# Input projection of a diffusion block: the order of weight loads, of the modulation's dot products and of the first tile

## The chip, the cores and the metric

The kernel runs on one core of a Trainium2 chip. Its time is the device time of one execution in microseconds (us); smaller is better. Runs of the kernel before are summed up by their median. The engines are named as the profile names them: PE multiplies matrices (PEld is its weight load), DVE and ACT work elementwise, POOL is the fourth compute engine, and SP issues transfers, which 16 DMA engines carry out. On-chip memory is SBUF (data) and PSUM (matmul results).

## The reference

One block of a diffusion transformer on 512 latent tokens and 256 context tokens, width 2048, all in float32. Cut to what the change touches:

```python
mod_l = silu(c) @ w_ada + b_ada            # 6 x 2048 values
mod_c = silu(c_ctx) @ w_ada + b_ada        # the same for the context
sh_a, sc_a, gt_a, sh_f, sc_f, gt_f = split(mod_l, 6)
h_l = rms_norm(x, g_mix) * (1 + sc_a) + sh_a       # 512 x 2048
h_c = rms_norm(ctx, g_mix) * (1 + csc_a) + csh_a   # 256 x 2048
p_l = h_l @ w_in                           # 2048 x 3904: query, key/value, rotary key, conv
p_c = h_c @ w_in                           # only its key/value columns are read later
# attention of latent tokens over latent and context keys; gated convolution of width 3
x = x + gt_a * (merge(att, conv) @ w_out)  # the output projection
x = x + gt_f * conv_ffn(modulate(rms_norm(x)), w_up, w_down)
out = rms_norm(x, g_final)
```

## The kernel before

Activations lie transposed: a tile holds 128 of the 2048 features (k = 0 to 15) by 512 tokens. Every product is made of three matmuls, high x high, high x low and low x high (`mm3`, L180), since each operand is split into a rounded high part (a cast on ACT) and the rest (a subtraction on DVE). For weights that is `split` (L156), with its cast at L164 and its low part at L165; for activations it is `hilo` (L312), at L315 and L316.

The input projection has 31 column tiles of 128 and goes through k in three chunks of 2, 4 and 10 tiles (`KCH`, index `ci`). Within a chunk, the first six column tiles (`G`) are worked row by row into six PSUM halves (`pf`), so that they can begin as soon as one k tile exists; the remaining 25 follow one by one (`pp`), and each is added to its sum `acc` by `evac` (ACT copies in the first chunk, L517; DVE adds later, L519). PSUM gives these tiles four single banks and two double ones in turn (`bank`). Weights arrive as `rf` (768 KB, for the six first tiles and two k) and `rw` (up to 1024 KB); both use the `raw` tag with two buffers, and their split parts `wh` and `wl` have four buffers and a spare for every fifth.

A tile of h (`prep`, L406) needs two values per feature out of w_ada: `mods` (L402) loads two tiles of w_ada for the scale (t = 16 + j) and for the shift (t = j), each as two halves 128x1024 (`ada`, 512 KB each, four buffers), and DVE multiplies each half by the vector `sv` (silu(c), on all 128 partitions) and sums it in one instruction (`dot_v`, L227). `modulate` (L410) then multiplies x by the norm's reciprocal root `rl`, and applies scale and shift on ACT (L416). Tiles 0 and 1 are made ahead of their matmuls in the first chunk, the others between column tiles by the table `todo`.

The norm's sum of squares is one chain of 16 additions on DVE (`add_squares`, L333). PE sums it over partitions (`rs`, L298), ACT takes the root (L275), DVE the reciprocal (L277), PE spreads it (L282), and ACT copies it to `rl` (L305). The vectors silu(c) and silu(c_ctx) come through `silu_rows` (L383): an 8 KB row is loaded, four matmuls against ones spread it over the partitions, and four Silu activations write `sv` or `svc`. ACT loads another function table (ACT_TABLE_LOAD) when it goes from Silu to the square root.

The context's scales and shifts are the same dots with `svc` (`ctx_mods`, L498, dots at L508): 32 steps of two dots, taken by `next(cm)`: one at each of the ten k rows of the third chunk's first tiles, then one at each following column tile and two at every fourth. `ctx_prep` (L483) makes two context tiles each from the results; `ctx_tile` (L659) multiplies them by w_in's key/value columns after the latent tokens are done (weights `wc`, PSUM `pc`).

A scheduler orders each engine's instructions with a timeline of its own; `keep` fixes some in program order. `fetch_to` (L141) keeps all loads on SP's queue in program order until the second chunk's first tiles are done (`ordered[0] = False`). SP issues one transfer after the other, and a load waits at the queue's head until its buffer is free. A weight load of `load` (L147) is written where its tile is wanted. `sv` is also stored to DRAM (`sv_d`, 1 MB), to be read back in the last part of the kernel. The output projection (around 640 to 700 us) also has a first part worked row by row with weights `ofr` (768 KB, split parts `ofw`), while `x` tiles are loaded again by `x_tile` (L947).

## Time and profile before

| | |
|---|---|
| time, median of 3 runs | 2158.85 us (2157.04 to 2159.15) |
| profiled execution's own time | 2154.39 us |
| its span in the trace | 2152.4 us |
| granted clock, mean | 0.995 |
| PE busy | 2092.9 us, 97% |
| DVE busy | 1770.2 us, 82% |
| ACT busy | 1047.3 us, 49% |
| first matmul of the projection | 30.12 us |
| first matmul of the second chunk | 85.19 us |
| first matmul of the third chunk | 170.24 us |

A row of a timeline reads: start, duration, engine, line, operation, result<-operands, and in brackets the idle time before it with what ended it. A row of waits reads: who waited, <-, for whom, then us in total, times, longest. SPq is SP's queue of issues. The profiled execution is one run; its time lies 4.5 us under the median.

### The profile page before, as it was taken

To read this page: it belongs to the slowest core of one execution; us is meant where nothing else is said; L and a number is where in the kernel's file an instruction comes from. 1 tells how busy PE (TensorE), PEld (TensorE's weight loads), DVE (VectorE), ACT (ScalarE), POOL (GpSimd) and SP (SyncE) were. 2 spreads that over 40 slices of the span, in tenths; PEclk is the share of its full clock that TensorE was granted. 3 is DMA by queue.
4 is the path that set the end of the run, shared out by engine and by line. 5 is a ranking of instruction groups with operands and counts; after the bars stand their busy time and mean duration, and the time that the engine had idled before them with its cause. 6 is when DMAs were issued, how large, how long until landed. Compare 5 with 4: busy or idle time off the path is not lost.

```text
span 2152.4 us, 37747 instructions
## 1 busy us (share of the span) xinstructions
PE 2092.9 (97%) x14458; PEld 1936.3 (90%) x14458; DVE 1770.2 (82%) x2859; ACT 1047.3 (49%) x1709; POOL 188.6 (9%) x270
## 2 busy tenths in 40 slices
PE   7899999999999999999999999999999989999997
PEld 4688788888888888999999999999999869999997
DVE  7998987778886989788888878888888658888886
ACT  5533333555552337555555555555555424333445
POOL 0000000000000000111211211211111000000000
PEclk9999999999999999999999999999999999999998
DMA  9989785334559976677877877887887998888782
GB/s 332 346 276 333 272 281 177 130 124 166 167 197 350 373 272 192 159 215 202 242 224 222 241 221 226 241 238 216 245 233 222 350 329 246 272 222 241 207 253 96
DMA packets 162410, 513.89 MB, mean 239 GB/s; under 512 B 18995, under 2 KB 23347, under 8 KB 156595
## 3 DMA queue, kind: packets, MB, share of 16 engines
q1 hardware_dynamic: 132564, 417.10, 56.9%
q0 software_dynamic: 27488, 92.29, 18.3%
q8 instruction: 113, 1.85, 0.4%
q10 hardware_dynamic: 2176, 2.10, 0.3%
q14 instruction: 69, 0.56, 0.1%
HBM read 464.22 MB, written 46.14 MB: 237 GB/s over the span
## 4 chain that ended last, share of the span: by engine, by line
PE 88%; DMA 5%; DVE 4%; issue 1%; ACT 1%; SPq 0%; POOL 0%; DVEq 0%; ACTq 0%; POOLq 0%
PE pp L181 4%; PE pp L183 4%; PE pp L182 4%; PE o L181 1%; PE o L183 1%; PE o L182 1%; DMA ada<-in_w_ada 1%; PE uf L181 1%; PE uf L182 1%; PE uf L183 1%; PE of L181 1%; PE of L182 1%; PE of L183 1%; PE pf L182 1%; PE pf L183 1%
## 5 line engine op out<-in xcount | busy, mean ns | idle before, releaser
L1029 POOL DMA_DIRECT2D t_d<-tp x126 | 72.7, 580 | 461.6 <-DVE tp L1028 458.7
L249 DVE SCALAR_TENSOR_TENSOR ada<-ada,sv 128x1024 f32<-128x1024 f32 x68 | 82.0, 1218 | 13.1 <-DMA ada<-in_w_ada 13.1
L164 ACT CAST w_0h<-rw 128x512 fp32r<-128x512 f32 (+1 forms) x63 | 38.3, 618 | 108.0 <-PE pp L182 63.6
L1106 POOL DMA_DIRECT2D u_s<-in_w_up x80 | 70.3, 879 | 226.4 <-DMA u_s<-in_w_up 124.8
L227 DVE SCALAR_TENSOR_TENSOR ada<-ada,sv 128x1024 f32<-128x1024 f32 x64 | 77.4, 1217 | 3.8 <-DMA ada<-in_w_ada 3.6
L508 DVE SCALAR_TENSOR_TENSOR ada<-ada,svc 128x1024 f32<-128x1024 f32 x64 | 75.8, 1218 | 3.2 <-DMA ada<-in_w_ada 3.2
L1027 ACT CAST tp<-a 128x256 fp32r<-128x256 f32 x90 | 34.8, 406 | 66.5 <-DMA t_d<-tp 58.0
L771 POOL TENSOR_TENSOR gr<-gr,half 128x8 f32<-128x8 f32 x4 | 10.1, 2522 | 629.3 <-DVE gr L770 537.0
L165 DVE TENSOR_TENSOR w_0l<-rw,w_0h 128x512 fp32r<-128x512 f32 (+1 forms) x63 | 42.5, 680 | 21.8 <-ACT w_0h L164 21.6
L249 DVE SCALAR_TENSOR_TENSOR ra<-ra,sv 128x1024 f32<-128x1024 f32 x44 | 52.4, 1216 | 1.3 <-DMA ra<-in_w_ada 1.3
L1198 DVE TENSOR_TENSOR u<-u,u_s 128x1024 f32<-128x1024 f32 x40 | 48.8, 1219 | 1.2 <-DMA u_s<-in_w_up 1.2
L1199 DVE TENSOR_TENSOR u<-u,u 128x1024 f32<-128x1024 f32 x40 | 48.7, 1217 | 0.0
L1028 DVE TENSOR_TENSOR tp<-a,tp 128x256 fp32r<-128x256 f32 x90 | 36.1, 417 | 13.5 <-ACT tp L1027 13.3
L742 ACT CAST pth<-t 128x384 fp32r<-128x384 f32 x64 | 28.6, 485 | 26.3 <-PE t L739 26.3
L1027 ACT CAST tp<-ts 128x256 fp32r<-128x256 f32 x36 | 14.6, 407 | 44.0 <-DMA t_d<-tp 42.2
L1028 DVE TENSOR_TENSOR tp<-ts,tp 128x256 fp32r<-128x256 f32 x36 | 15.1, 421 | 25.2 <-ACT tp L1027 25.2
L519 DVE TENSOR_TENSOR acc<-acc,pp 128x512 f32<-128x512 f32 x50 | 34.0, 679 | 2.1 <-PE pp L183 2.1
L743 DVE TENSOR_TENSOR ptl<-t,pth 128x384 fp32r<-128x384 f32 x64 | 33.2, 548 | 2.7 <-ACT pth L742 2.7
L723 DVE TENSOR_REDUCE mn<-s 128x1 f32<-128x768 f32 x32 | 30.3, 951 | 4.8 <-PE s L712 4.6
L990 ACT ACTIVATE g<-cg,sm 128x512 f32<-128x512 f32 x40 | 32.5, 813 | 1.0 <-DVE cg L1167 0.9
L990 ACT ACTIVATE a<-ca,sm 128x512 f32<-128x512 f32 x40 | 32.1, 802 | 0.0
L1233 DVE SCALAR_TENSOR_TENSOR aq<-aq,svq 128x512 f32<-128x512 f32 x32 | 21.1, 688 | 12.6 <-DMA aq<-in_w_ada 11.2
(15965 smaller groups left out, 9380.6 us busy)
## 6 DMA issues: line engine op xcount, KB each, us to landing
ada<-in_w_ada SPq DMA_DIRECT2D x196, 512.0 KB, 5.8
u<-in_w_up SPq DMA_DIRECT2D x120, 512.0 KB, 8.2
w<-t_d SPq DMA_DIRECT2D x161, 256.0 KB, 4.3
u_s<-in_w_up SPq DMA_DIRECT2D x80, 512.0 KB, 4.2
u_s<-in_w_up POOLq DMA_DIRECT2D x80, 512.0 KB, 9.1
t_d<-tp POOLq DMA_DIRECT2D x126, 256.0 KB, 5.0
v<-in_w_dnw SPq DMA_DIRECT2D x72, 384.0 KB, 4.6
ra<-in_w_ada SPq DMA_DIRECT2D x22, 1024.0 KB, 4.9
```

The costliest lines, as they stand in the source:

```text
L181: PE.matmul(ps, w[0], x[0], start=first, stop=False, skip_group_check=on_top)
L182: PE.matmul(ps, w[0], x[1], start=False, stop=False, skip_group_check=on_top)
L183: PE.matmul(ps, w[1], x[0], start=False, stop=last, skip_group_check=on_top)
L227: V.scalar_tensor_tensor(out=r, in0=r, scalar=1.0, in1=vec[:, i * 1024:(i + 1) * 1024], op0=ALU.mult, op1=ALU.mult, accum_out=col[:, i:i + 1])
L249: keep(V.scalar_tensor_tensor(out=r, in0=r, scalar=1.0, in1=svs[i], op0=ALU.mult, op1=ALU.mult, accum_out=lc[:, t % 4:t % 4 + 1] if i else ...
L508: keep(V.scalar_tensor_tensor(out=raw[q], in0=raw[q], scalar=1.0, in1=svc[:, q * 1024:(q + 1) * 1024], op0=ALU.mult, op1=ALU.mult, accum_o ...
L990: A.activation(u, src, AF.Identity, bias=s("fb", m), scale=s("fw", 86 + m))
L1027: A.copy(out=z[:, :256], in_=src)
L1028: V.tensor_tensor(out=z[:, 256:], in0=src, in1=z[:, :256].bitcast(F32), op=ALU.subtract)
L1029: G_.dma_start(t_d[p, OPS.index(n)], z.bitcast(F32))
L1106: G_.dma_start(r[-1], src[more], accum_op=ALU.add)
L1198: V.tensor_tensor(out=a11, in0=a11, in1=s1, op=ALU.add)
```

## The change

Five things change.

1. The weight loads of the projection stand in a table, and `weights()` hands out the load that was issued one step earlier and issues the next. In the first chunk the next one is issued after the second tile's modulation loads.
2. The first tile has its own code. Its two pairs of w_ada tiles are loaded and the scale's dots (t = 16) come ahead of the reciprocal; the shift's dots (t = 0) are put around the multiplication by `rl`. The squares are summed in two chains of eight. Casts and low parts of the first weights are ordered after named instructions by `issue_after`, and the copy of `rl` comes ahead of the weights' casts.
3. The context's row is no longer loaded at the beginning and spread by matmuls. In the second chunk, after the first tiles, c_ctx is loaded to all 128 partitions (1 MB) and one Silu of 128x2048 makes `svc`.
4. The context's dots: one step at the first eight rows of the third chunk's first tiles, then one at each column tile. `ctx_prep` begins two tiles later.
5. The store of `sv` goes from the beginning to the output projection, behind the seventh x tile.

```diff
@@ split
-        A.copy(out=hi[:, :n], in_=raw[:, a:a + n])
-        V.tensor_tensor(out=lo[:, :n], in0=raw[:, a:a + n], in1=hi[:, :n].bitcast(F32), op=ALU.subtract)
+        with tc.issue_after(cast_after[0]) if cast_after else ExitStack():
+            last_hi[:] = [A.copy(out=hi[:, :n], in_=raw[:, a:a + n]).ins]
+        with tc.issue_after(low_after[0]) if low_after else ExitStack():
+            V.tensor_tensor(out=lo[:, :n], in0=raw[:, a:a + n], in1=hi[:, :n].bitcast(F32), op=ALU.subtract)
@@ the first tile
+        def first_scale():
+            first["raw"] = [ada_load(t) for t in (16, 0)]
+            first["col"] = [tiny(2, f"dv{t}") for t in (16, 0)]
+            for i in range(2):
+                first["last"] = first_dot(0, i)
+            total(first["col"][0], 16, mod[:, 16:17])
...
+        def prep_first():
+            a = first_dot(1, 0, recips[0])
+            with tc.issue_after(a):
+                b = V.tensor_tensor(out=xs[0], in0=xs[0], in1=rl, op=ALU.mult).ins
+            first_dot(1, 1, b)
+            low_after[:] = [total(first["col"][1], 0, mod[:, 0:1]).ins]
...
-            ssq = add_squares(ssq, xs[j], T, f"xs{j}")
-        silu_rows(c_ctx, svc, "cc")
+            ssq = add_squares(ssq if j % 8 else None, xs[j], T, f"xs{j}")
+            if j % 8 == 7:
+                sqs.append(ssq)
         fetch_to(sm, small)
-        rms([ssq], D, T, rl)
+        first_scale()
+        ahead.append(first["last"])
+        rms(sqs, D, T, rl)
@@ the three chunks
+        def load_next():
+            if loads:
+                a, k = loads.popleft()
+                ready.append(load(w_in[:, a:a + k], k, f"rw{a}"))
+
+        def weights(ahead=True):
+            raw = ready.popleft()
+            if ahead:
+                load_next()
+            return raw
+
+        load_next()
...
-                    prep(q)
+                    prep(q) if q else prep_first()
+                    if q:
+                        load_next()
                 elif ci == 2:
                     if q in (2, 4):
                         modulate(13 + q // 2)
-                    next(cm)
+                    if q < 8:
+                        next(cm)
                     pump(1)
                 if q % 2 == 0:
-                    raw = load(w_in[:, off:off + 2 * G * P], 2 * G * P, f"rf{ci}{q}")
+                    raw = weights(ci > 0)
...
+                fetch_to(svc, c_ctx.to_broadcast([P, D]))
+                A.activation(svc, svc, AF.Silu)
                 fetch_to(kc, consts[:, :KCW])
...
                 if i % per == 0:
-                    k = min(per, len(ORDER) - G - i) * n
-                    raw = load(w_in[:, off:off + k * P], k * P, f"rw{ci}_{m}")
-                    off += k * P
+                    raw = weights()
...
                 if ci == 2:
-                    for q in range(2 if i % 4 == 0 else 1):
-                        next(cm, None)
-                    if i >= 5 and i % 2 == 1 and (i - 5) // 2 < CTX_EARLY:
-                        bg.append(ctx_prep((i - 5) // 2))
+                    next(cm, None)
+                    if i >= 7 and i % 2 == 1 and (i - 7) // 2 < CTX_EARLY:
+                        bg.append(ctx_prep((i - 7) // 2))
@@ output projection
-        SP.dma_start(xres[m], xt[:, m * T:(m + 1) * T])
+        ins = SP.dma_start(xres[m], xt[:, m * T:(m + 1) * T]).ins
+        if m == 6:
+            with tc.issue_after(ins):
+                SP.dma_start(sv_d, sv)
...
-    SP.dma_start(sv_d, sv)
```

The order of SP's transfers around the first weights, before (`rf` and `rw` are weights, `ada` halves of modulation tiles; all rows go through one helper line):

```order
25 L143 DMA rf_251<-in_w_in 128x1536
26 L970 DMA sv_d<-sv 128x2048
27 L143 DMA ada_283<-in_w_ada 128x1024
28 L143 DMA ada_285<-in_w_ada 128x1024
29 L143 DMA ada_291<-in_w_ada 128x1024
30 L143 DMA ada_293<-in_w_ada 128x1024
31 L143 DMA rw_13_337<-in_w_in 128x2048
...
39 L143 DMA ada_459<-in_w_ada 128x1024
40 L143 DMA rw_21_473<-in_w_in 128x2048
```

And with the change, where all weights are called `rw`:

```order
24 L143 DMA rw_226<-in_w_in 128x1536
25 L143 DMA ada_274<-in_w_ada 128x1024
...
28 L143 DMA ada_284<-in_w_ada 128x1024
29 L143 DMA rw_298<-in_w_in 128x2048
30 L143 DMA rw_330<-in_w_in 128x2048
31 L143 DMA ada_353<-in_w_ada 128x1024
...
38 L143 DMA ada_452<-in_w_ada 128x1024
39 L143 DMA rw_466<-in_w_in 128x2048
```

The second large load moved from behind eight halves of modulation tiles to right behind the first, the third took its old place, and the store of `sv` is gone from here.

DVE around the reciprocal of the first norm, before (L227 are dots, L165 low parts of weights, L413 is x times `rl`):

```order
19 L227 SCALAR_TENSOR_TENSOR ada_227,dvl_231<-ada_227,sv 128x1024
20 L227 SCALAR_TENSOR_TENSOR ada_229,dvl_231<-ada_229,sv 128x1024
...
22 L227 SCALAR_TENSOR_TENSOR ada_235,dvl_239<-ada_235,sv 128x1024
...
24 L227 SCALAR_TENSOR_TENSOR ada_237,dvl_239<-ada_237,sv 128x1024
25 L221 SCALAR_TENSOR_TENSOR mod<-dvl_239,sm 128x1
26 L277 RECIPROCAL rr<-rr 128x4
27 L165 TENSOR_TENSOR wf_0l<-rf_251,wf_0h 128x512
28 L165 TENSOR_TENSOR wf_4l<-rf_251,wf_4h 128x512
29 L165 TENSOR_TENSOR wf_8l<-rf_251,wf_8h 128x512
30 L413 TENSOR_TENSOR xr_113<-xr_113,rl 128x512
```

And with the change (L428 are the first tile's dots, L434 its product with `rl`):

```order
18 L428 SCALAR_TENSOR_TENSOR ada_192,dv_200<-ada_192,sv 128x1024
19 L428 SCALAR_TENSOR_TENSOR ada_194,dv_200<-ada_194,sv 128x1024
20 L285 RECIPROCAL rr<-rr 128x4
...
22 L428 SCALAR_TENSOR_TENSOR ada_196,dv_201<-ada_196,sv 128x1024
...
24 L434 TENSOR_TENSOR xr_113<-xr_113,rl 128x512
25 L428 SCALAR_TENSOR_TENSOR ada_198,dv_201<-ada_198,sv 128x1024
26 L227 SCALAR_TENSOR_TENSOR mod<-dv_201,sm 128x1
27 L167 TENSOR_TENSOR wf_0l<-rw_226,wf_0h 128x512
```

The reciprocal stands behind two dots and no longer four, and the product with `rl` stands ahead of the weights' low parts.

DVE at the end of the projection, before (L519 adds the last column tile, L165 with `wc` are low parts of the context's weights, L316 with q00l belongs to the first query product):

```order
537 L322 TENSOR_TENSOR hc_3406<-cr_3403,hc_3406 128x256
538 L316 TENSOR_TENSOR q00l<-pq_3423,q00h 128x512
539 L165 TENSOR_TENSOR wc_0l<-rc_3530,wc_0h 128x512
540 L519 TENSOR_TENSOR acc_710<-acc_710,pp_29_3259 128x512
541 L165 TENSOR_TENSOR wc_0l<-rc_3530,wc_0h 128x512
542 L452 TENSOR_TENSOR acc_710<-acc_710,acc_695 128x512
```

And with the change (L548 are context dots, L533 and L335 make context tiles):

```order
519 L559 TENSOR_TENSOR acc_703<-acc_703,pp_29_3235 128x512
520 L548 SCALAR_TENSOR_TENSOR ada_3267,modc<-ada_3267,svc 128x1024
521 L548 SCALAR_TENSOR_TENSOR ada_3269,lcc<-ada_3269,svc 128x1024
...
523 L167 TENSOR_TENSOR wc_0l<-rc_3523,wc_0h 128x512
...
538 L533 TENSOR_TENSOR cr_3390<-cg_3384,rc 128x256
539 L533 TENSOR_TENSOR cr_3396<-cg_3384,rc 128x256
540 L335 TENSOR_TENSOR hc_3393<-cr_3390,hc_3393 128x256
541 L335 TENSOR_TENSOR hc_3399<-cr_3396,hc_3399 128x256
542 L327 TENSOR_TENSOR q00l<-pq_3416,q00h 128x512
```

Two context dots and six context tiles with their splits (the last pair is shown) now stand behind that column tile, ahead of the low part of the first query product.

More of the change, by code (lines that the diff above doesn't have):

```diff
@@ L226, in dot_v @@
         for i, r in enumerate(raw):
-            V.scalar_tensor_tensor(out=r, in0=r, scalar=1.0, in1=vec[:, i * 1024:(i + 1) * 1024], op0=ALU.mult, op1=ALU.mult, accum_out=col[:, i:i + 1])
+            with tc.issue_after(last_lo[0]) if t in (1, 17, 2, 18) else ExitStack():
+                V.scalar_tensor_tensor(out=r, in0=r, scalar=1.0, in1=vec[:, i * 1024:(i + 1) * 1024], op0=ALU.mult, op1=ALU.mult, accum_out=col[:, i:i + 1])
         total(col, t, dst)
@@ L276, in rsqrt @@
         roots[:] = roots[-1:] + [ins.ins]
-        V.reciprocal(r, r)
+        with tc.issue_after(ahead.pop()) if ahead else ExitStack():
+            recips[:] = [V.reciprocal(r, r).ins]
+    recips, ahead = [], []
     def spread(pb, r):
@@ L412, in modulate @@
             xr = xs[j]
-            keep(V.tensor_tensor(out=xr, in0=xr, in1=rl, op=ALU.mult))
+            if j:
+                keep(V.tensor_tensor(out=xr, in0=xr, in1=rl, op=ALU.mult))
             sc = tiny(1, f"sc{j}")
@@ L422, in block_kernel @@
         xs = []
-        ssq = None
+        ssq, sqs = None, []
         for j in range(NK):
@@ L540, in block_kernel @@
         todo[1, 22] = [(prep, 13)]
-        off = 0
+        loads, off = deque(), 0
+        for n in KCH:
+            per = max(1, 2048 // (n * P))
+            for k in [2 * G] * (n // 2) + [min(per, len(ORDER) - G - i) * n for i in range(0, len(ORDER) - G, per)]:
+                loads.append((off, k * P))
+                off += k * P
+        ready = deque()
+        def load_next():
[8 more added lines that the diff above has]
+        load_next()
         for ci, (k0, n) in enumerate(zip(K0, KCH)):
```

23 lines of the change are left out of this document (19 added, 4 removed).

## The prediction

> **What bounds the kernel now.** I read the page first, its engine shares and its chain of waits:
>
> ```profile
> PE 2092.9 (97%) x14458; PEld 1936.3 (90%) x14458; DVE 1770.2 (82%) x2859; ACT 1047.3 (49%) x1709; POOL 188.6 (9%) x270
> PE 88%; DMA 5%; DVE 4%; issue 1%; ACT 1%; SPq 0%; POOL 0%; DVEq 0%; ACTq 0%; POOLq 0%
> ```
>
> PE is the path, and an edit pays only where PE stands. So next comes the table of windows over the first k-chunk, then one of the same stage as a whole (columns: window, its length, busy time of PE, PEld, DVE, ACT and POOL with instruction counts, granted clock, DMA share, GB/s):
>
> ```profile
> 24.00:36.00 12.00, 8.11 (x28) 6.16 (x27) 9.44 (x21) 5.54 (x9) 0.00 (x0) 1.00 1.01 403
> 84.00:96.00 12.00, 12.00 (x53) 9.73 (x52) 11.73 (x24) 7.79 (x15) 0.00 (x0) 1.00 1.01 403
> 24.00:84.00 60.00, 47.16 (x185) 35.21 (x185) 51.11 (x104) 32.13 (x58) 0.00 (x0) 1.00 0.90 330
> ```
>
> From 84 us PE is full; before that it is not, while DMA is at 0.90 and DVE at 51.11 of 60. PE's timeline has the stage's ends and the pace of a matmul:
>
> ```profile
> 16.16 7.16 PE L391 MATMUL cc<-cc,io 1*128 1x512 f32 x8 [4.65 <-DMA cc<-in_c_ctx]
> 23.25 1.87 PE L298 MATMUL rs<-io,xs0t 128*128 128x1 f32 x8
> 30.12 1.22 PE L181 MATMUL pf<-h0h,wf_0h 128*128 128x512 f32 x2 [3.21 <-ACT h0h L315]
> 32.42 0.63 PE L182 MATMUL pf<-h0l,wf_0h 128*128 128x512 f32 x1
> 32.84 0.63 PE L183 MATMUL pf<-h0h,wf_0l 128*128 128x512 f32 x1
> 85.19 0.40 PE L181 MATMUL pf<-h2h,wf_0h 128*128 128x512 f32 x1
> 85.89 0.39 PE L181 MATMUL pf<-h3h,wf_4h 128*128 128x512 f32 x1
> ```
>
> The last two rows are three matmuls apart: 0.233 us each. The chunk has 31 tiles x 2 rows x 3 = 186 matmuls, 43.3 us of work, and takes 85.19 - 30.12 = 55.07: PE loses 11.8 us in it, and starts only at 30.12. The views of waits between 24 and 90 us, of PE, ACT, DVE and SP, and ACT's timeline say on what:
>
> ```profile
> PE pp L181 <- ACT acc L517: 7.4, 6, 2.3
> ACT w_0h L164 <- DMA rw<-in_w_in: 6.4, 1, 6.4
> DVE ada L227 <- DMA ada<-in_w_ada: 3.6, 4, 1.4
> DVE w_0l L165 <- ACT w_0h L164: 2.8, 2, 1.5
> SPq L143 <- DVE ada L227: 38.0, 20, 4.6
> 53.79 0.62 ACT L164 CAST w_0h<-rw 128x512 fp32r<-128x512 f32 x1 [6.38 <-DMA rw<-in_w_in]
> ```
>
> SP stands 38.0 us behind modulation buffers that DVE has yet to read, and the weights' load stands behind those in SP's queue. ACT then waits 6.38 us for weights, its evacuations wait behind that cast, and PE waits for a bank. Without lost waits DVE would be next: 8.9 us idle is all it has.
>
> **The first tile.** ACT's and DVE's timelines before the first matmul, and the DMA issues between 10 and 55 us:
>
> ```profile
> 23.97 1.28 ACT L275 ACT_TABLE_LOAD   x1
> 26.46 0.62 ACT L164 CAST wf_8h<-rf 128x512 fp32r<-128x512 f32 x1
> 26.98 0.58 ACT L305 COPY rl<-rs 128x512 f32<-128x512 f32 x1
> 29.45 0.62 ACT L315 CAST h0h<-xr 128x512 fp32r<-128x512 f32 x1
> 18.57 0.69 DVE L333 TENSOR_TENSOR xs0t<-xs0t,xs 128x512 f32<-128x512 f32 x1
> 25.56 0.18 DVE L277 RECIPROCAL rr<-rr 128x4 f32<-128x4 f32 x1 [1.14 <-ACT rr L275]
> rf<-in_w_in SPq DMA_DIRECT2D x1, 768.0 KB, 8.2
> sv_d<-sv SPq DMA_DIRECT2D x1, 1024.0 KB
> ```
>
> The sum of squares is complete at 19.3, but PE is in the context row until 23.3 and only then starts rs. That row goes. rs starts near 19.3, the table load no longer stands behind four Silus, and the reciprocal comes near 21.8, behind the two dots of t=16 (2.4). Then the path is another: COPY rl ends near 23.5, while the first weights land at 23.8 (issued at 15.6, 8.2 to land; without the 1 MB of sv_d beside them perhaps 1 us sooner). Three casts, 0.52 apart, bring 25.4; xr times rl, the second dot and its total bring the shift near 25.5; xr on ACT 0.81 and h0h 0.62, and the first matmul follows h0h's start by 30.12 - 29.45 = 0.67: about 26.9. **Term 1: -3.2 us** (from -1.5, if the weights land as before and the casts wait, to -4.5).
>
> Before those matmuls PE rests some 4 us, as it rested 3.21 before; the first eight stand 0.43 apart (32.42 to 32.84) against 0.233 later, 1.5 us that I leave as they are. The Trainium skill ("TensorE: Matmul & The Clock Gate", Part 1) speaks against taking the context's eight matmuls away: the array runs at half clock until it has been busy for about 3.4 us, and the start of that window varies from run to run. By the trace those matmuls did not keep the clock up; by the page the slow stretch could be one more or less half window, some 1.5 us either way as an estimate, and the sum would stand between -6.2 and -3.2.
>
> **Weights one ahead.** The load that landed at 53.8 is now issued right behind the one before it, near 30 us; one 1024 KB load took 9.3 here, so it lies ready by 40. ACT's 6.4 goes, and with it the waits of PE that follow from it (2.33 and 1.59 of the 7.4). The other four of the six stay, since they are evacuations in turn of two double banks; ACT's order now also puts xr and a cast ahead of one evacuation, some 1.1. **Term 2: -2.8 us** (0 to -5). The second chunk then starts near 79.2. Terms 1 and 2 together leave DVE 3 us of its 8.9 idle, so they can't be much larger.
>
> **The context's row.** The load is 1 MB now, as one of rw, and comes in the second chunk beside a full PE:
>
> ```profile
> 86.00:130.00 44.00, 44.00 (x191) 35.68 (x190) 43.73 (x83) 17.86 (x31) 0.00 (x0) 1.00 0.86 313
> PE pp L183 <- DVE w_0l L165: 1.6, 1, 1.6
> ```
>
> ACT gets two table loads of 1.28 and a Silu of four times 0.60 at most, 5 us of 26 idle; the next cast behind them is wanted only after the first six tiles, 18 us into the chunk. Its reader is the third chunk, from 170 us. Term 3: 0. If the cover failed, the landing (4.9 to 9.3 for 1 MB) less that lead would still be under 2.
>
> **Dots spread evenly.** The only stall in 130 to 240 us is the second row above, with two dots in one step ahead of a low part. **Term 4: -1.6 us** (0 to -1.7). But 14 dots now come after 353 us. What lies there:
>
> ```profile
> L508 DVE SCALAR_TENSOR_TENSOR ada<-ada,svc 128x1024 f32<-128x1024 f32 x64 | 75.8, 1218 | 3.2 <-DMA ada<-in_w_ada 3.2
> 353.00:363.00 10.00, 10.00 (x47) 7.97 (x46) 6.05 (x15) 2.69 (x6) 0.00 (x0) 1.00 0.45 131
> 363.00:373.00 10.00, 10.00 (x46) 8.14 (x46) 5.96 (x12) 3.97 (x8) 0.00 (x0) 1.00 0.22 66
> 383.00:393.00 10.00, 10.00 (x47) 8.15 (x45) 8.65 (x17) 6.30 (x13) 0.00 (x0) 1.00 0.31 101
> 393.00:403.00 10.00, 10.00 (x47) 8.19 (x47) 7.35 (x17) 6.03 (x13) 0.00 (x0) 1.00 0.74 266
> 403.40 0.68 DVE L165 TENSOR_TENSOR wc_0l<-rc,wc_0h 128x512 fp32r<-128x512 f32 x1
> 410.87 0.29 PE L181 MATMUL pc<-hc,wc_0h 128*128 128x256 f32 x1
> 411.96 0.28 PE L181 MATMUL pc<-hc,wc_0h 128*128 128x256 f32 x1
> ```
>
> Fourteen dots, 1.15 apart, are 16.1 us; DVE's idle time from 353 to 410 is about 15.1 (10 less its busy time in each such window), in pieces behind ACT. The last two dots stand behind the evacuation of the last column tile, with six context tiles, their splits and the low parts of wc behind them, and PE's pc waits for those. DVE led by 410.87 - 404.1 = 6.8 us. Counted from the last column tile's end, PE now has 34 matmuls of pq (7.9 us), qr with its wait (some 2) and 36 of pc, 0.12 apart (410.87 to 411.96 for nine), 4.4: 14.3 us until it needs a low part of the second context tile. DVE has some 30 operations in its order ahead of that part, two dots of 1.15 and the others 0.4 to 0.7 each, some 15, and about 1.5 of hand-overs with ACT: 16.4. **Term 5: +2.1 us** (0 if the idle time is usable, +9.3 = 16.1 - 6.8 if none is).
>
> **sv_d.** The store now stands among the x loads of the output projection. The windows there, ACT's waits between 655 and 690 us, its cast, and PE's use of it:
>
> ```profile
> 670.00:680.00 10.00, 10.00 (x44) 8.10 (x43) 3.62 (x7) 1.66 (x3) 0.00 (x0) 1.00 1.04 404
> ACT ofw_0h L164 <- DMA ofr<-in_w_out_first: 23.5, 4, 13.4
> 674.92 0.62 ACT L164 CAST ofw_0h<-ofr 128x512 fp32r<-128x512 f32 x1 [13.43 <-DMA ofr<-in_w_out_first]
> 676.77 0.40 PE L181 MATMUL of<-mx12h,ofw_0h 128*128 128x512 f32 x1
> ```
>
> DMA is saturated and the weights lead PE by 1.85 us. At 404 GB/s the store's 1.05 MB less one x tile (0.26 MB) that now comes behind is 2.0 us, plus its issue and the store's own landing: the weights come about 2.6 late. **Term 6: +0.8 us** (0 if the store falls in a gap, +2.6 if nothing leads).
>
> **Sum.** -3.2 - 2.8 + 0 - 1.6 + 2.1 + 0.8 = -4.7 us, against the profiled execution's own 2154.39 (span 2152.4): 2149.7. That execution lies 4.5 below the median of the runs, 2158.85; a comparison goes by medians, so I predict 2158.85 - 4.7 = 2154.2 us. A difference under 0.2%, 4.3 us, can't be told from none here.
>
> **Rivals.** A, as summed: 0.42, own range 2151 to 2157.5. B, modulation tiles become the wait: one MB moved ahead of ada tiles makes DVE's 3.6 us of DMA waits double. For it: DMA at 1.01 in the first window, four ada buffers only. Against: sv_d's 1 MB leaves just that stretch. DVE's idle would then be 8.9 - 1.1 (reciprocal) - 2.8 + 3.6 = 8.6, the second chunk would start at 84.9, and with terms 4 to 6 the sum is -0.3 - 1.6 + 2.1 + 0.8 = +1.0: 2159.9, chance 0.22. C, the context's dots at the end put DVE late: none of its 15.1 us is usable, term 5 is +9.3; it decides from 7 us on, where all gains are spent, and gives -4.7 - 2.1 + 9.3 = +2.5, 2161.4; with term 1 and 2 at their lower ends too, 2164. For it: the idle pieces are hand-overs from ACT. Against: 4 us idle in each of the windows from 353 to 373, where PE is paced by itself. Chance 0.18. D, the late costs vanish: terms 5 and 6 at 0, -7.6, and 2 somewhat larger, 2150; chance 0.18. That the store costs nothing alone is inside A.
>
> Faster comes from D wholly, from A a little over half and from a sliver of B: 0.45. Slower comes from near half of C and tails of A and B: 0.16. Same: 0.39. The range leaves out the far ends of C and D: 2147 to 2162.5.
>
> **What would show it.** In the changed profile: first pf matmul near 27 (term 1); no wait of ACT for rw between 40 and 60, and the second chunk's first pf near 79 (2); ACT's svc in 80 to 95 with no idle PE (3); no wait of PE at 222 less the shift (4); PE's first pc about 2 us later against the end of the last column tile than now, with a wait ended by DVE (5); one wait of PE on ofw in the output projection under 1 us (6). Wrong is the forecast if the second chunk starts after 83, if PE waits over 5 us between 390 and 420, or if a stage that the diff does not touch moves by over 2 us, which the trace of before cannot show.

## The result

The changed kernel takes 2171.62 us (median of 4 runs, 2169.35 to 2175.38), the kernel before 2159.0 (4 runs beside them): a ratio of 1.0061, 95% interval 1.0043 to 1.008. It is 12.6 us slower, where 4.7 us faster was forecast. Both its engine shares and its chain of waits still name PE:

```profile
PE 2100.3 (97%) x14458; PEld 1947.2 (90%) x14458; DVE 1769.7 (82%) x2858; ACT 1049.4 (48%) x1708; POOL 188.1 (9%) x270
PE 91%; DMA 4%; DVE 3%; ACT 1%; issue 1%; SPq 0%; DVEq 0%; ACTq 0%; POOLq 0%
```

DVE's work has not grown. PE's busy time is 7.4 us longer with the same 14458 matmuls, but that can't be put down to the change: a second profile of the kernel before reads 2100.9. To see where the time comes from, the start of the first PE matmul of each stage is put side by side. The third column of the table is that second profile, taken beside the experiments; its execution took 2159.59 us, like the median, while the first one took 2154.39.

| first PE matmul of | before, us | before again | changed | changed less before again |
|---|---|---|---|---|
| the projection (pf) | 30.1 | 29.5 | 26.9 | -2.7 |
| second chunk | 85.2 | 84.0 | 81.4 | -2.6 |
| third chunk | 170.2 | 169.4 | 166.7 | -2.7 |
| query product (pq) | 393.4 | 392.6 | 387.6 | -4.9 |
| rotary product (qr) | 407.1 | 406.3 | 413.7 | +7.4 |
| context tiles (pc) | 410.9 | 410.0 | 419.8 | +9.7 |
| output projection (of) | 624.7 | 625.9 | 634.7 | +8.7 |
| up projection (uf) | 812.1 | 812.7 | 823.3 | +10.6 |
| down projection (d) | 1679.0 | 1683.9 | 1695.2 | +11.3 |
| the last matmul | 2141.2 | 2146.4 | 2157.4 | +11.0 |

Up to the query product the change wins 4.9 us; between it and the context tiles, within 32 us, it loses 14.6; nothing before or after is of that size. The view of PE's waits over the whole changed kernel has two rows that were not there, or small, before, those on xq and on wq02h (some rows are left out):

```profile
PE qr L370 <- ACT xq L701: 8.2, 1, 8.2
...
PE pp L187 <- ACT acc L557: 5.5, 5, 1.9
PE pf L187 <- ACT h0h L326: 4.3, 1, 4.3
...
PE pq L187 <- ACT wq02h L165: 3.3, 1, 3.3
```

In the kernel before the wait on xq was there already, as a short one. Its PE timeline:

```profile
405.77 0.39 PE L183 MATMUL pq<-qa3h,wq02l 128*128 128x512 f32 x1
407.12 1.13 PE L357 MATMUL qr<-xq,kc 128*128 128x512 f32 x2 [0.97 <-ACT xq L630]
```

The same place in the changed kernel, timelines of PE, ACT and DVE:

```profile
413.69 2.07 PE L370 MATMUL qr<-xq,kc 128*128 128x512 f32 x2 [8.19 <-ACT xq L701]
416.41 0.63 PE L189 MATMUL pq<-qa0h,wq01l 128*128 128x512 f32 x1
416.84 0.63 PE L187 MATMUL pq<-qa1h,wq01h 128*128 128x512 f32 x1
...
405.82 1.09 ACT L534 ACTIVATE cr<-cr,modc,scc 128x256 f32<-128x256 f32 x2
...
408.43 1.09 ACT L534 ACTIVATE cr<-cr,modc,scc 128x256 f32<-128x256 f32 x2 [0.93 <-DVE cr L533]
...
410.98 1.09 ACT L534 ACTIVATE cr<-cr,modc,scc 128x256 f32<-128x256 f32 x2 [0.86 <-DVE cr L533]
...
413.06 0.58 ACT L701 COPY xq<-pq 128x512 f32<-128x512 f32 x1
...
401.03 1.22 DVE L548 SCALAR_TENSOR_TENSOR ada<-ada,svc 128x1024 f32<-128x1024 f32 x1
402.17 1.22 DVE L548 SCALAR_TENSOR_TENSOR ada<-ada,svc 128x1024 f32<-128x1024 f32 x1
...
407.98 0.75 DVE L533 TENSOR_TENSOR cr<-cg,rc 128x256 f32<-128x256 f32 x2
...
410.53 0.75 DVE L533 TENSOR_TENSOR cr<-cg,rc 128x256 f32<-128x256 f32 x2
```

PE has finished its product at 405.5 and wants xq, a copy of 0.58 us. On ACT that copy stands behind six context tiles; the last four of these wait for DVE's products cr, and DVE does those after the last two dots, at 401 and 402. When PE starts again, its matmuls stand 0.43 us apart (416.41 to 416.84) and not 0.233: from 413.69 to pc it needs 6.1 us for what took 3.8 before. The wait of 3.3 us on wq02h, at 391 us, is followed by such a stretch too; its eight matmuls take 3.5 us, where they would take 1.9 at the full pace. So 14.4 of the 14.6 us are told: 7.2 more on xq, 3.3 on wq02h, and 3.9 of half pace behind the two.

### The profile page after: what moved, and what is told of

Its sections match the earlier page's. It is cut to its first block, busy times and chain, and to the rows that moved or that the text cites. A ratio compares the mean times of both kernels' runs of the same rounds, so it can differ in the third digit from the quotient of the medians.

```text
span 2168.3 us, 37708 instructions
## 1 busy us (share of the span) xinstructions
PE 2100.3 (97%) x14458; PEld 1947.2 (90%) x14458; DVE 1769.7 (82%) x2858; ACT 1049.4 (48%) x1708; POOL 188.1 (9%) x270
## 4 chain that ended last, share of the span: by engine, by line
PE 91%; DMA 4%; DVE 3%; ACT 1%; issue 1%; SPq 0%; DVEq 0%; ACTq 0%; POOLq 0%
PE pp L187 4%; PE pp L188 4%; PE pp L189 4%; DMA ada<-in_w_ada 1%; PE d L187 1%; PE o L187 1%; PE o L188 1%; PE d L188 1%; PE o L189 1%; PE d L189 1%; PE uf L187 1%; PE uf L188 1%; PE uf L189 1%; PE of L187 1%; PE of L188 1%; PE of L189 1%
## 5 line engine op out<-in xcount | busy, mean ns | idle before, releaser
L256 DVE SCALAR_TENSOR_TENSOR ada<-ada,sv 128x1024 f32<-128x1024 f32 x68 | 82.2, 1219 | 14.3 <-DMA ada<-in_w_ada 14.2
L165 ACT CAST w_0h<-rw 128x512 fp32r<-128x512 f32 (+1 forms) x63 | 38.4, 617 | 106.2 <-PE pp L188 63.9
L548 DVE SCALAR_TENSOR_TENSOR ada<-ada,svc 128x1024 f32<-128x1024 f32 x64 | 75.8, 1218 | 0.5 <-DMA ada<-in_w_ada 0.5
L234 DVE SCALAR_TENSOR_TENSOR ada<-ada,sv 128x1024 f32<-128x1024 f32 x60 | 72.6, 1221 | 2.6 <-DMA ada<-in_w_ada 2.4
L1100 ACT CAST tp<-ts 128x256 fp32r<-128x256 f32 x36 | 14.6, 407 | 43.2 <-DMA t_d<-tp 39.1
L1101 DVE TENSOR_TENSOR tp<-ts,tp 128x256 fp32r<-128x256 f32 x36 | 15.1, 421 | 23.0 <-ACT tp L1100 23.0
L1306 DVE SCALAR_TENSOR_TENSOR aq<-aq,svq 128x512 f32<-128x512 f32 x32 | 21.0, 688 | 14.9 <-DMA aq<-in_w_ada 14.0
```

The source lines that it names most:

```text
L234: V.scalar_tensor_tensor(out=r, in0=r, scalar=1.0, in1=vec[:, i * 1024:(i + 1) * 1024], op0=ALU.mult, op1=ALU.mult, accum_out=col[:, i:i + 1])
L256: keep(V.scalar_tensor_tensor(out=r, in0=r, scalar=1.0, in1=svs[i], op0=ALU.mult, op1=ALU.mult, accum_out=lc[:, t % 4:t % 4 + 1] if i else ...
L548: keep(V.scalar_tensor_tensor(out=raw[q], in0=raw[q], scalar=1.0, in1=svc[:, q * 1024:(q + 1) * 1024], op0=ALU.mult, op1=ALU.mult, accum_o ...
L1100: A.copy(out=z[:, :256], in_=src)
L1101: V.tensor_tensor(out=z[:, 256:], in0=src, in1=z[:, :256].bitcast(F32), op=ALU.subtract)
```

## The experiments

The columns give the second chunk's start, then how each kernel's starts stand to the second profile of before (us, minus is earlier), and the timed ratio to before with its interval.

| kernel | second chunk | at pq | at pc | at uf | ratio |
|---|---|---|---|---|---|
| changed | 81.4 | -4.9 | +9.7 | +10.6 | 1.0061 (1.0043 to 1.008) |
| dots_as_before | 82.0 | -1.6 | -1.6 | +3.2 | 1.0014 (1.0002 to 1.0026) |
| dots_alone | 83.4 | -2.5 | +12.4 | +15.7 | 1.0063 (1.0046 to 1.0081) |
| ctx_tiles_3 | 82.2 | -4.0 | -0.9, then +10.9 | +17.0 | 1.0083 (1.0066 to 1.01) |
| warm_14 | 82.3 | -2.0 | +12.0 | +15.8 | 1.0066 (1.0049 to 1.0083) |
| dots_mid | 82.6 | -2.6 | +4.5 | +6.5 | 1.0028 (1.0016 to 1.0041) |
| short_dots | 81.6 | -3.4 | +0.3 | +5.4 | 1.0012 (0.9995 to 1.0029) |
| store_as_before | 79.0 | -7.0 | +9.3 | +9.2 | 1.0036 (1.002 to 1.0051) |
| dots_store_as_before | 78.5 | -4.2 | -4.2 | -0.6 | 0.9996 (0.9982 to 1.001) |
| loads_and_tile | 86.6 | +6.3 | +6.3 | +6.9 | 1.0017 (1.0003 to 1.003) |
| loads_alone | 80.7 | -2.0 | -2.0 | -1.3 | 1.0013 (1.0 to 1.0026) |
| tile_alone | 88.9 | +6.5 | +6.5 | +8.6 | 1.0032 (1.0018 to 1.0046) |
| best_try | 80.2 | -3.1 | -3.1 | -3.9 | 0.9986 (0.9968 to 1.0004) |

### The dots undone, and the dots alone

`dots_as_before` is the changed kernel with

```diff
-                    if q < 8:
-                        next(cm)
+                    next(cm)
...
-                    next(cm, None)
-                    if i >= 7 and i % 2 == 1 and (i - 7) // 2 < CTX_EARLY:
-                        bg.append(ctx_prep((i - 7) // 2))
+                    for q in range(2 if i % 4 == 0 else 1):
+                        next(cm, None)
+                    if i >= 5 and i % 2 == 1 and (i - 5) // 2 < CTX_EARLY:
+                        bg.append(ctx_prep((i - 5) // 2))
```

> The changed kernel with one part undone: the context's dots and context tiles come at their old steps (two dots at every fourth column tile, first context tile after the fifth). Theory T, the even dots make the loss: they put six context tiles' activations ahead of the copy xq on ACT, and the query weights' loads behind modulation loads on SP. Then PE's waits on wq02 (3.3 us) and all but 1 us of that on xq (8.2) go, with 2 us of slow clock behind them, and the stall near 218 us comes back (1.6): some 11 to 13 us under the changed kernel, so 1 to 4 us under the kernel before. Rival R, the loads issued one ahead do it, because they fill SP's queue at the end of the projection: the waits stay, and the time is within 3 us of the changed kernel.

`dots_alone` is the kernel before with the same lines the other way round.

> The kernel before with that one part alone: even dots, context tiles two column tiles later. T: the wait of PE on xq appears here too, 7 us or more, the stall at 222 us goes (1.7): 8 to 14 us over the kernel before. R: no such wait, 0 to 2 us under the kernel before.

PE's waits between 385 and 425 us, first with the dots undone, then with the dots alone:

```profile
PE qr L370 <- ACT xq L701: 1.0, 1, 1.0
```

```profile
PE qr L357 <- ACT xq L630: 8.2, 1, 8.2
PE pq L181 <- ACT wq02h L164: 3.2, 1, 3.2
```

The one part, late dots together with the later begin of the context tiles, makes the whole loss between pq and pc: 14.9 us by itself, 14.6 in the changed kernel, 0 without it. The rival is out: with the loads still one ahead, nothing is lost there. The query weights' lateness (3.2 us) belongs to the dots too. What was not met is the total of `dots_as_before`: 10.6 us under the changed kernel but still 1.4 parts in a thousand over the kernel before, though it is 1.6 us ahead of it at pc; a part of that is the store's, as shown below.

### What it is in the dots

`dots_mid` ends the dots at column tile 20 (before 17, changed 24; counted from 0):

```diff
-                    next(cm, None)
+                    for _ in range(2 if i % 6 == 0 else 1):
+                        next(cm, None)
```

> The changed kernel with one size between: two steps of dots at every sixth column tile, so that the last stands at column tile 20 of 24 (before: 17, changed: 24). Theory L, the loss at the end is the work that comes late, whatever engine shows the wait: four of the seven late steps, 9.2 us of dots, are gone from the end, so the shift between the first query product and pc falls from +14.6 to 3 to 8 us. Rival Q, one thing in the order on ACT makes it (the copy xq behind six context tiles' activations, an order that all such kernels have): the wait of PE on xq stays at 6 us or more.

`short_dots` keeps every step, load and queue, and takes the work out of the last seven steps, so that a part of the context's modulation is missing in what it computes:

```diff
+                    w = 1024 if i < 25 else 8
-                    keep(V.scalar_tensor_tensor(out=raw[q], in0=raw[q], ..., accum_out=d))
+                    keep(V.scalar_tensor_tensor(out=raw[q][:, :w], in0=raw[q][:, :w], ..., accum_out=d))
```

> The changed kernel, whose last 14 dots (seven steps) run over 8 columns instead of 1024, so that part of the context's modulation is left out; loads, queues and the order of the steps stay. It takes some 15 us of DVE's work from the end and nothing else. L with DVE as the cause: PE's waits on wq02 and xq fall together from 11.5 to under 4 us, and the time comes to within 3 us of the run with the old dots (2161). If the loads on SP's queue are the cause, which wait for buffers and not for DVE's time, the wait on wq02 stays at 2 us or more.

`ctx_tiles_3` leaves the dots and moves three pairs of context tiles behind the query products (`CTX_EARLY = 3`).

> The changed kernel with three instead of six pairs of context tiles made ahead of the first query products; the dots stay evenly spread. It moves three pairs' activations on ACT behind xq. T with ACT's queue as the cause of the 8.2 us: PE's wait on xq falls under 2.5 us, the wait on wq02 (3.3, from SP's queue) stays, and PE waits instead for context tiles in pc, 1 to 5 us: 4 to 8 us under the changed kernel. If the lateness of the dots on DVE sets the end, and not the order on ACT, the wait only moves to pc, and the time is within 2 us of the changed kernel.

PE's waits behind 385 us in the three, in this order:

```profile
PE qr L370 <- ACT xq L702: 5.6, 1, 5.6
```

```profile
PE qr L370 <- ACT xq L702: 3.0, 1, 3.0
```

```profile
PE pc L187 <- ACT hc L334: 5.4, 2, 3.2
PE pc L189 <- DVE wc_0l L167: 1.6, 2, 1.1
PE pq L187 <- ACT wq02h L165: 1.2, 1, 1.2
PE qr L370 <- ACT xq L701: 1.0, 1, 1.0
```

Between pq and pc, seven late steps cost 14.6 us. The four of `dots_mid` cost 7.1; I expected three there, but by the edit the steps behind column tile 17 are two at tile 18 and one each at 19 and 20. That is 1.8 to 2.1 us for each step of two dots, which DVE does in 2.3, and the three steps between the two kernels make 7.5 us for 6.9 us of dots. Without the dots' work, with all their loads, 3.7 is left, and the wait on wq02 is gone: SP's queue was waiting for buffers that DVE freed late. So DVE's late time makes 10.9 of the 14.6 us. The 5.6 us of wait in `dots_mid` alone would hardly have ruled out rival Q, a fixed order on ACT with 6 us or more; the 3.0 of `short_dots`, whose steps stand in the same places, does. The 3.7 that stay are 2.0 us more of the wait on xq and 1.6 of half pace behind it. What makes them was not tried: all of these kernels also begin the context tiles two column tiles later, and no run undoes that alone.

The order on ACT only decides where the wait shows. With three pairs of tiles moved away the wait on xq falls to 1.0, as my theory said, but PE then waits for the context tiles and the low parts in pc, and by the first key products (pkl) the kernel is 10.9 us late, later than the changed one there (9.2). My expectation of 4 to 8 us won was wrong; it was the second of the two expected outcomes, and worse.

`store_as_before` gives the same reading from another side: it reaches pq 2.1 us earlier than the changed kernel, and pc at 419.4 against 419.8. PE waits 10.3 us for xq in place of 8.2. So in this pair the end of the stage is set by DVE and ACT, and not by when PE comes there.

### The store, the loads, the first tile

`store_as_before` and `dots_store_as_before` are the changed kernel and `dots_as_before` with

```diff
-        ins = SP.dma_start(xres[m], xt[:, m * T:(m + 1) * T]).ins
-        if m == 6:
-            with tc.issue_after(ins):
-                SP.dma_start(sv_d, sv)
+        SP.dma_start(xres[m], xt[:, m * T:(m + 1) * T])
...
+    SP.dma_start(sv_d, sv)
```

> The changed kernel with the store of sv at the beginning again, and nothing else. The two runs with old dots differ by 3.5 us in the first chunk (78.5 against 82.0) with this store as their only difference. Theory O, the store moves DVE's order in the first chunk (a sum and a scale factor stand later, ACT waits 6.7 us for the latter, PE 2.3 us, and its pace halves for eight matmuls): here too the second chunk starts at 78 to 79.5 in place of 81.4, the end is unchanged, and the total is 2 to 4 us under the changed kernel. Rival, it was chance of one execution: second chunk at 81 to 82.5.

> The changed kernel with two parts undone: the context's dots at their old steps, and the store of sv at the beginning again. Theory S, the store's new place costs in the output projection: that part gets 1 to 3 us shorter than in the run with the old dots alone, and the total 2157 to 2159, under the kernel before. Rival, the store costs nothing there and helped at the beginning: the first projection matmul comes 0 to 1 us later than 26.8, and the total stays within 1.5 us of the run with the old dots alone (2161).

ACT's timeline near 72 us in `store_as_before`:

```profile
71.13 1.54 ACT L557 COPY acc<-pp 128x512 f32<-128x512 f32 x3
73.34 0.62 ACT L165 CAST wf_0h<-rw 128x512 fp32r<-128x512 f32 x1 [0.66 <-DMA rw<-in_w_in]
```

The same two steps in the changed kernel, and PE behind them:

```profile
71.75 0.62 ACT L165 CAST wf_0h<-rw 128x512 fp32r<-128x512 f32 x1 [1.24 <-DMA rw<-in_w_in]
72.28 1.56 ACT L557 COPY acc<-pp 128x512 f32<-128x512 f32 x3
72.91 0.50 PE L187 MATMUL pp<-h0h,w_0h 128*128 128x512 f32 x1 [1.92 <-ACT acc L557]
```

The store's new place costs 2.4 us in the first chunk (81.4 against 79.0; 3.5 in the pair with old dots), some 590 us before the transfer itself runs (at 669). Theory O's figure for the second chunk was met, but it named the wrong place: ACT's wait of 6.7 us, at the second tile, is the same in both kernels, and up to 70 us the changed one is even 0.7 us ahead. The loss comes at 72 us. The scheduler orders by its own timeline, and without the store in it the cast of the next weights stands ahead of three evacuations on ACT. It waits for its load, the evacuations wait behind it, and PE loses 1.9 us to the other kernel there and 1.2 more in seven gaps at half pace. In all six kernels with the late store that were profiled beside the changed one or are it (changed, dots_as_before, ctx_tiles_3, warm_14, dots_mid, short_dots) that cast waits ahead of the evacuations, and PE falls to half pace near 74 us; in the three with the new first tile, a late context row and the early store (store_as_before, dots_store_as_before, best_try) the evacuations come first, and it does not.

In the output projection the store costs nothing: the shift at its first matmul and at the end of its first part is the same, +9.92 us against the first profile of before. The total of `dots_store_as_before`, 2156.94 us, is the one that theory S named, but by luck: what it wins lies in the first chunk.

`loads_alone` is the kernel before with the table of loads, `tile_alone` with the first tile's code, and `loads_and_tile` has both; in all three the context's row stays at the beginning. The core of their differences is in the change shown above.

> The kernel before with the weight loads issued one ahead, and nothing else. Theory of the prediction: ACT's wait of 6.4 us for weights goes, with the waits of 2.3 and 1.6 us of PE, and the second chunk starts 2 to 3 us earlier than 85.2. Rival, DVE sets the end of the first chunk (51 us busy of 60 before): PE's waits only move to other evacuations, and the second chunk starts at 84 to 86. Either way the later parts keep what is won: total 2156 to 2160.

> The kernel before with the first tile's new order alone (dots ahead of the reciprocal, two sums of squares, casts and low parts ordered by name). Theory: with the context's row still there the first matmul comes at 28 to 29.5; as the weights' load at 44 us is as late as before, the second chunk starts no more than 1 us earlier. Rival: the whole gain in the first chunk is from this part, second chunk at 82 to 83.

> Loads one ahead and the first tile's new order alone; dots, store and the context's row as before. Theory: the context's row at the beginning holds rs back to 23.3 us, so that the first projection matmul comes at 28 to 29.5 in place of 26.8, and the total is 1 to 2 us over that of the run with the row late and dots and store early. Rival: the row is hidden either way (the first weights land at 23.8), first matmul under 27.5.

In the first chunk the loads do what was forecast: ACT's wait of 6.4 us is gone, and the second chunk starts at 80.7, 3.3 us before the second profile's 84.0. The total does not follow: 2162.59 us, over the 2156 to 2160 that were expected and 3 us over the kernel before, though the profiled execution is 1.3 us ahead at the up projection. Why stays open. The first tile alone is a loss, where a gain was expected. Timelines of PE, ACT and DVE of `tile_alone`:

```profile
16.29 7.16 PE L404 MATMUL cc<-cc,io 1*128 1x512 f32 x8 [4.52 <-DMA cc<-in_c_ctx]
23.38 1.87 PE L309 MATMUL rs<-io,xs0t 128*128 128x1 f32 x8
25.10 1.84 PE L309 MATMUL rs<-io,xs8t 128*128 128x1 f32 x8
32.93 1.65 PE L187 MATMUL pf<-h0h,wf_0h 128*128 128x512 f32 x3 [4.30 <-ACT h0h L326]
...
26.99 0.26 ACT L282 ACTIVATE rr<-rs,eps 128x4 f32<-128x4 f32 x1
31.41 0.81 ACT L453 ACTIVATE xr<-xr,mod,sc 128x512 f32<-128x512 f32 x1 [2.16 <-DVE mod L227]
...
27.28 0.18 DVE L285 RECIPROCAL rr<-rr 128x4 f32<-128x4 f32 x1 [5.50 <-ACT rr L282]
29.89 1.22 DVE L428 SCALAR_TENSOR_TENSOR ada<-ada,sv 128x1024 f32<-128x1024 f32 x1
```

With the context's row ahead of it, rs runs from 23.4 to 26.9 us. It is twice as long as before, since there are two sums of squares and PE could take neither while it was in the row; so the reciprocal comes at 27.3, against 25.6 in the first profile of before, whose context row started at the same time (16.2). That is 1.7 us. DVE stands idle for 5.5 us ahead of it, because the shift's two dots were put behind the reciprocal by name; they follow on the path and cost the other 1.1: first matmul at 32.9, against 30.1. Against the second profile (29.5) the loss is 3.4. The new first tile is worth something only with the late row, where the first sum is done long before the second; there the first matmul comes at 26.9. `loads_and_tile` has the same first matmul as `tile_alone`, 32.9, and not the 28 to 29.5 that were expected; its total is 4.4 us over that of `dots_store_as_before`, and not 1 to 2.

### A bridge of matmuls, and a last try

`warm_14` puts 14 matmuls of constants between the norm's spread and the first projection matmul (the trace has two records for each):

```diff
+        warm = sml("warm")
+        after_t = last_t[0]
+        for _ in range(14):
+            with tc.issue_after(after_t):
+                after_t = PE.matmul(warm[:, :P], ident, ones, start=True, stop=True).ins
```

> The changed kernel with 14 matmuls of constants (128x128, read by nobody) put on PE between the norm's spread and the first projection matmul, a gap of 4.3 us in which PE rested. Theory C: after that rest the first 13 matmuls stand 0.43 us apart, because PE was idle; kept busy, they stand 0.23 apart, and the first chunk gets 1.5 to 3 us shorter, as much of it kept by the end of the projection as DVE and the evacuations allow (1 to 2.5 us). Rival: the pace comes from the time since the start or from the data, and nothing changes but PE's own issue: within 0.5 us of the changed kernel in the first chunk.

PE's timeline in `warm_14`:

```profile
22.65 4.40 PE L476 MATMUL warm<-io 128*128 128x128 f32 x28
28.41 0.40 PE L189 MATMUL pf<-h0l,wf_0h 128*128 128x512 f32 x1
28.65 0.40 PE L190 MATMUL pf<-h0h,wf_0l 128*128 128x512 f32 x1
35.34 1.22 PE L188 MATMUL pf<-h1h,wf_4h 128*128 128x512 f32 x2 [3.74 <-ACT h1h L327]
37.64 0.63 PE L188 MATMUL pp<-h0h,w_0h 128*128 128x512 f32 x1
38.06 0.63 PE L189 MATMUL pp<-h0l,w_0h 128*128 128x512 f32 x1
```

Kept busy, PE starts at full pace (28.41 to 28.65: 0.24 us). But it then runs dry sooner, waits 3.7 us for h1h, and is slow after that (37.64 to 38.06). The second chunk starts at 82.3, no earlier than without. Half pace follows a rest of PE, as theory C said; taking it away won nothing here. PE had to wait for h1 in any case, and h1 was no earlier: DVE has the scale for it at 33.6 us, against 33.3 in the changed kernel.

`best_try` is `dots_store_as_before` with one step of dots and not two at the third chunk's first column tile (`2 if i % 4 == 0 and i else 1`).

> Loads one ahead, the first tile's order and the late context row, with store and dots at their old places, except that the first column tile of the third chunk takes one step of dots and not two (its 2.0 us wait of PE near 218 us was the cost of even one double step there); the last dot then stands at column tile 18 in place of 17. Theory L prices one step later at the end at up to 2.3 us, and the wait near 218 at 1.7 to 2: the shift at pc stays -4 to -7 us against the kernel before. In the total, if what is won before 440 us is kept, 2151 to 2155; if the norm behind the output projection gives 3 us of it back again, as in the run with the old dots and store (its reciprocal stood behind dots that waited for transfers), 2155 to 2158.

The wait near 218 us stays at 2.0, so the double step there is not its cause. The shift at pc is -3.1, not the expected -4 to -7; the total is in the range for the case that some is given back. The last dots stand one step later than in the kernel before, and between pq and pc nothing is lost: one late step is free here, where the context tiles begin at their old step. Its median is 2157.0 against 2160.82, 0.9986 with an interval that reaches 1.0004, so that no gain at all is possible too. No version beat the kernel before beyond doubt, while this one and `dots_store_as_before` (2156.94) lie some 14 us under the changed kernel.

`before_again` is the kernel before, unchanged.

> The kernel before once more, for a second profile: which stretches at half pace and which pace of the up projection belong to an execution and not to a kernel. If they belong to the execution, this profile has a slow stretch near 620 us or a pace of 120.0 ns in place of 118.7 between 1290 and 1680 us, though the kernel is the same; if they belong to the changes, it repeats the first profile within 1 us at all marks.

That second profile repeats the first within 1.2 us up to 1300 us and is then 5 us later at the end, with no wait of PE in between. The windows there, of the first and the second profile of the same kernel:

```profile
1300.00:1400.00 100.00, 100.00 (x845) 100.00 (x844) 84.40 (x116) 58.55 (x91) 19.31 (x29) 1.00 0.81 231
```

```profile
1300.00:1400.00 100.00, 100.00 (x836) 100.00 (x835) 83.52 (x115) 58.48 (x89) 19.32 (x29) 1.00 0.80 228
```

One per cent more matmuls in the same time, at a granted clock that reads 1.00 in both. The pace belongs to the execution. It is about as large as the 4.5 us by which the first profile lay under the median, and as the gap between the 16 us that the two first profiles differ by and the 12.6 of the medians.

## Why the prediction was wrong

**Term 5 failed**, the 14 dots after 353 us: +2.1 forecast, 0 to +9.3 as its bounds, +14.6 measured (387.6 to 419.8 against 392.6 to 410.0). The prediction's own sign for it, over 5 us of PE waiting between 390 and 420, came: 8.2.

First, the lead was wrong. I took DVE's 6.8 us between wc's low part and pc, and from the last column tile's end I gave PE 14.3 us until it needs DVE. But PE wants xq before that, and its timeline of before had the row: a wait of 0.97 us at 407.12, no lead at all. In the changed kernel PE wants xq 5.1 us after that column tile (400.4 to 405.5), while DVE and ACT need 12.6 us to get there (400.43 to 413.06). I priced the operation that DVE does last and not the first one that PE waits for; the order of ACT, where xq stands behind the context tiles, I left out.

Second, the count began at the end of the last column tile. DVE came there without a backlog (its addition starts as PE's last matmul ends, at 400.4), but 4.8 us had been lost before: the wait on wq02h and the half pace behind it. The other 2.3 us of half pace, behind xq, I had not priced either.

Third, the two bounds, all of DVE's idle time usable or none of it, both miss. By `short_dots`, some 15 us of late dots cost 10.9, of which 2.3 are half pace; so the idle time (15.4 us by the windows, 15.1 in my sum) took up somewhat under half of them. Rival C had the nearer mechanism (late DVE, decided from 7 us on) and 18 in 100, but called the idle time wholly unusable and had the same wrong lead, so that even it ended at 2161.4. Its worst case is also wrongly added: with terms 1 and 2 at their lower ends it is 2165.9, not 2164.

**Term 1** was right: -3.2 forecast, -3.2 against the first profile and -2.7 against the second, with the reciprocal at 21.24 (forecast 21.8), the first cast at 23.53 (23.8) and the first matmul at 26.88 (26.9). From DVE's, ACT's and PE's timelines of the changed kernel:

```profile
21.24 0.18 DVE L285 RECIPROCAL rr<-rr 128x4 f32<-128x4 f32 x1
23.53 0.62 ACT L165 CAST wf_0h<-rw 128x512 fp32r<-128x512 f32 x1 [0.32 <-DMA rw<-in_w_in]
26.88 1.65 PE L187 MATMUL pf<-h0h,wf_0h 128*128 128x512 f32 x3 [4.29 <-ACT h0h L326]
```

The experiments add its condition: without the late row the same code costs 2.8 us against the first profile and 3.4 against the second.

**Term 2** was right in its mechanism and missed in the sum: ACT's wait of 6.4 us is gone, but the second chunk began at 81.4 and not at 79.2. The missing 2.2 us are the store's: with it at its old place the chunk starts at 79.0. The changed kernel's granted clock in the stage is 0.97, where it was 1.00, and in the stage of term 5 it is 0.86:

```profile
24.00:84.00 60.00, 50.64 (x192) 38.70 (x193) 54.00 (x109) 32.58 (x60) 0.00 (x0) 0.97 0.91 334
376.00:424.00 48.00, 36.56 (x162) 29.27 (x161) 38.05 (x79) 20.09 (x39) 0.00 (x0) 0.86 0.47 154
```

**Term 3** was right: 0, no wait of PE in the second chunk. **Term 4** was right in its number and wrong in its cause: -1.6 forecast; the stall went, and the kernel won 2.2 us between the third chunk's start and pq. But I put the stall down to the double step there, and `best_try` has no double step and keeps it. In the 8 us ahead of that low part DVE does three dots in `best_try` and one in the changed kernel, which leaves out the steps at the last two rows; that these are the cause is argued, not tried. **Term 6** was 0 and not +0.8 where I put it, and +2.4 where I had priced nothing, in the first chunk, as an order that the scheduler made: an edit that moves one transfer moved instructions some 590 us away from it.

**Rival B** did not come: DVE waited 2.4 us for modulation tiles in that stage, where it had waited 3.6. The Trainium skill ("TensorE: Matmul & The Clock Gate", Part 1) says that the number of slow matmuls depends on where in a free-running window the first one lands, so that one kernel has more or fewer of them from run to run. The traces agree: among the first tile's matmuls, after rests of 3.2 to 4.3 us, there are 6 gaps of 0.43 us in the first profile of before, 10 in the second and 12 in the changed one. Six gaps more are 1.2 us, within the 1.5 us either way that I had weighed.

**The rest of the loss** is small and only partly explained. From the output projection's first part to the up projection the changed kernel loses 1.9 us more, and `dots_store_as_before` gives back 3.5 of its 4.1 us between 694 and 812. In its trace (`dots_store_as_before`) the norm's reciprocal there stands on DVE behind dots whose tiles arrive late:

```profile
801.02 1.22 DVE L256 SCALAR_TENSOR_TENSOR ada<-ada,sv 128x1024 f32<-128x1024 f32 x1 [1.50 <-DMA ada<-in_w_ada]
804.48 1.23 DVE L256 SCALAR_TENSOR_TENSOR ada<-ada,sv 128x1024 f32<-128x1024 f32 x1 [0.60 <-DMA ada<-in_w_ada]
805.63 0.16 DVE L285 RECIPROCAL rr<-rr 128x2 f32<-128x2 f32 x1
```

The kernel before has the same picture, a reciprocal at 806.6 behind dots that waited 1.0 and 0.4 us, so the view does not single out a cause. Whether the order or the transfers make the difference was not tried, and stays open.

## What to carry to other kernels

Work that is moved late on an engine is not simply paid by that engine's idle time when that time is hand-overs with another engine (here some 15 us of late dots cost 10.9): price it one for one until a measurement says less. The lead that counts is that of the first thing the bounding engine waits for, found by walking every queue that this thing passes (here a copy of 0.58 us on ACT, behind six tiles), and a wait of 1 us already there means no lead. A kernel whose order a scheduler makes answers to an edit far from it: compare the orders over the whole program, and test parts in pairs, since one (the first tile) may pay only with another (the late row).

## What the runs showed of the hardware

After a rest of PE of 3.2 to 8.2 us its 512-column matmuls stand 0.43 us apart in place of 0.233, for 6 to 12 gaps in a row. Near 74 us in the changed kernel the same pace came for seven gaps behind a rest of 1.9 us, the longest of four (0.7 to 1.9) within 20 us; without that one, in `store_as_before`, it did not come. The granted clock there, and behind the wait on xq:

```profile
73.90:77.30 3.40, 3.40 (x9) 2.64 (x9) 3.36 (x9) 0.00 (x0) 0.00 (x0) 0.50 1.00 387
408.50:418.50 10.00, 4.82 (x9) 3.15 (x10) 5.10 (x12) 4.89 (x11) 0.00 (x0) 0.50 0.01 2
```

The column before the last two reads 0.50, half the clock. Between 27 and 32 us, where matmuls of the first tile stand 0.43 us apart as well, the view reads 1.00, so at the start of this trace it does not show the pace.

In the up projection two executions of one kernel ran 1% apart in pace (845 and 836 matmuls in 100 us) from 1290 to 1680 us while the granted clock read 1.00 in both; that alone is 4 us, nearly the whole gain that was forecast.
